# First norm's gain as one row spread by TensorE, a TensorE start at the first microseconds, S5 table loads issued one by one, rotary angles in two steps

## The chip, the cores and the metric

The kernel runs on one core of one Trainium2 chip. The metric is the device time of one execution in microseconds, the median of the runs shown.

## The reference

Two layers of a hybrid decoder trunk on 256 tokens of width 1024, all in float32. What matters here, cut short:

```python
for l in range(2):
    h = _rmsnorm(x, ffn1_norm[l])
    x = x + 0.5 * _swiglu(h, ffn1_w_gate[l], ffn1_w_up[l], ffn1_w_down[l])   # 1024 -> 2816 -> 1024
    h = _rmsnorm(x, mix_norm[l])
    ... = jnp.split(h @ w_in[l], IN_SPLIT_POINTS, axis=-1)                   # 1024 -> 12288
    y_a = _hgrn2(...); y_b = _s5(...); y_c = _conformer_conv(...); y_d = _dilated_attention(...)
    merged = sum over k of gates[:, :, k] * (y_k @ w_branch[l, k])
    x = x + merged @ w_out[l]
    h = _rmsnorm(x, ffn2_norm[l])
    x = x + 0.5 * _swiglu(h, ffn2_w_gate[l], ffn2_w_up[l], ffn2_w_down[l])
return _rmsnorm(x, final_norm)

def _rmsnorm(x, gain):
    return x * lax.rsqrt(jnp.mean(x * x, axis=-1, keepdims=True) + 1e-6) * gain
```

The S5 mixer needs, per layer, tables made from its parameters alone (powers of the diagonal state matrix, `b` and `c` folded into them); the attention's partial rotary embedding needs cosines and sines of position times 16 frequencies.

## The kernel before

**Work and stages.** The 256 tokens are two row tiles of 128. TensorE multiplies activations by 270 MB of weights, streamed once. A float32 weight slot of 128x1024 elements arrives in a buffer `raw`; ScalarE rounds it to a high part `whi`, VectorE forms the rest `wlo`; each activation is split the same way (`hTh`, `hTl`), and each product is the sum of three matmuls, `hi*hi`, `hi*lo` and `lo*hi` (`mm3`). One slot is used by 12 matmuls of 512 columns or 24 of 256. `Stream` keeps up to 4 loads (`NRAW`) and 5 slots (`NW`) split ahead of TensorE. Weight loads are issued on SyncE's queue (SP, L139).

**What sets the order.** All is written into the engines' streams by one Python program, in order. `Paced` adds up estimated times for each engine as instructions are written; side jobs (generators: `prepare`, the S5 tables, the mixers) are advanced by `tick` between matmuls where those estimates leave room. A side job's bare `yield` lets it go on once TensorE's estimated time has caught up with what the job wrote; `yield n` waits at least 2.6 us times n of that time; `yield GO` lets it go on at once if there is room. So a change of a yield or of an instruction moves side jobs among the matmuls of one feed-forward stage.

**The start.** SP loads `x[0]` in two halves (L391), then `gain0`, the first norm's gain repeated over 128 partitions by a zero-stride read (`load_gain`, L403), then two loads of the gate weights, `x[1]` (L408) and two more. `norm.square` squares and sums on ScalarE, `norm.rows` makes the scale `var` (GpSimd's power) and on VectorE `xn = x * var * gain`, in two halves of 512 columns; `norm.turn` transposes `xn` on TensorE into `xT`, which ScalarE and VectorE split into `hTh` and `hTl`; then the gate product (`gate_t`) of the first row tile goes over the four slots of the first 512 columns. The second row tile is normed between them, on the same engines.

**Side jobs in the first feed-forward.** `prepare` turns parameter columns, makes masks, the rotary angles `ang` (32 VectorE instructions of one column each) and the S5 constants. Then `s5_turns` (`ctab`, `stab`) and `s5_tables(l)`: seven loads issued by ScalarE without a yield between them (`braw` L632, `craw` L634, `draw` L635), then on VectorE `pows`, `bb`, `b` and `C4`, on TensorE transposes and small products `s5k`, and at last `K4` (named `K`, 20 instructions from `s5k`, then two additions). The second layer does its tables in its own first feed-forward. `K4` is first used by `s5()` in the mixers, whose products are `yk`.

PSUM's mixed banks (`mx_bank`, `tr_bank`: four buffers under one tag) hold transposes and side jobs' products; four others (`acc_bank`) the main products.

Of the kernel before, what the change touches and what calls it, by code (L numbers as in the profile page):

```python
# [16 lines left out]
ALU = mybir.AluOpType  # L17
AX = mybir.AxisListType

P = 128  # L20
DM = 1024
# [11 lines left out]
GO = -1  # L33
# [155 lines left out]
def trunk(ctx, tc, x_in, positions, ffn1_norm, ffn1_w_gate, ffn1_w_up, ffn1_w_down, mix_norm, w_in,  # L189
# [3 lines left out]
    nc = tc.nc  # L193
    V, S, T, G = (Paced(nc.vector, dve_cost), Paced(nc.scalar, ActCost()), Paced(nc.tensor, pe_cost),
                  Paced(nc.gpsimd, pool_cost))
# [5 lines left out]
    def const(shape, name, dtype=F32):  # L201
        return sb.tile(shape, dtype, tag=name, name=name, bufs=1)

    def H(shape, name, dtype=F32):
        return sb.tile(shape, dtype, tag="heap", name=name, bufs=NHEAP)

    def H2(shape, name, dtype=F32):
        return sb.tile(shape, dtype, tag="half", name=name, bufs=NHALF)
# [9 lines left out]
    def mx_bank(name):  # L218
        return ps.tile([P, 512], F32, tag="mx", name=name, bufs=4)

    def tiny(shape, name, bufs=4):
        return sb.tile(shape, F32, tag=name, name=name, bufs=bufs)
# [163 lines left out]
    ident = const([P, P], "ident")  # L386
    make_identity(nc, ident)

    x = [const([P, DM], f"x{t}") for t in range(2)]
# [3 lines left out]
    gain_src = []  # L393
# [3 lines left out]
    gains = {}  # L397

    def load_gain(n):
        if n < len(gain_src) and n not in gains:  # L400
            g = H([P, DM], f"gain{n}")
            src = gain_src[n]
            (nc.scalar if n else nc.sync).dma_start(g, bass.AP(tensor=src.tensor, offset=src.offset, ap=[[0, P], [1, DM]]))  # L403
            gains[n] = g

    load_gain(0)
    ws.load(2)
    nc.sync.dma_start(x[1], x_in[0, P:2 * P, :])  # L408
    ws.load()
# [69 lines left out]
    def prepare():  # L479
# [40 lines left out]
        pcol = tiny([P, 2], "pcol", 1)  # L520
        V.tensor_copy(pcol, b[:, :2])

        inv = np.float32(500000.0) ** (-np.arange(16, dtype=np.float32) / np.float32(16))
        ang = H2([P, 2, 2, 16], "ang")
        for i in range(16):
            for t in range(2):
                V.tensor_scalar(ang[:, t, 0, i:i + 1], pcol[:, t:t + 1], float(inv[i]), None, op0=ALU.mult)
            if i % 4 == 3:
                yield GO
        V.tensor_scalar(ang[:, :, 1, :], ang[:, :, 0, :], math.pi / 2, None, op0=ALU.add)  # L530

        red = H2([P, 2, 16], "red")
        src = H2([P, 2, 16], "angc")
# [27 lines left out]
        def t5(name):  # L561
            if name in ("mag", "cth", "sth", "zr", "zi"):
                return const([P, 32], "s5" + name)
            return t5t[:, t5n.setdefault(name, len(t5n)), :]
# [8 lines left out]
        hs, hc, ab = t5("hs"), t5("hc"), t5("ab")  # L573
# [47 lines left out]
    def s5_tables(l):  # L621
# [8 lines left out]
        draw = tiny([16, 2, 16], "draw", 1)  # L630
        for k, (bs, cs) in enumerate(((s5_b_re, s5_c_re), (s5_b_im, s5_c_im))):
            nc.scalar.dma_start(braw[:, k], bs[l].rearrange("(j g) p c -> (g p) j c", g=2))  # L632
            for g in range(2):
                nc.scalar.dma_start(craw[k][:, :, g, :], cs[l].rearrange("(a g) c p -> (g c) a p", a=4))  # L634
        nc.scalar.dma_start(draw, s5_d[l].rearrange("(a h c) -> h a c", a=2, c=16))  # L635
        yield

# [33 lines left out]
        for half in range(2):  # L671
            hs = slice(4 * half, 4 * half + 4)
# [34 lines left out]
        for half in range(2):  # L707
            hs = slice(8 * half, 8 * half + 8)
# [47 lines left out]
        for g in range(2):  # L756
            bv = kb[g].rearrange("p (h s c) -> p s h c", h=8, s=4)
            for i in range(4):
                for i0 in range(i + 1):
                    if i0 == 0:  # L760
                        V.tensor_scalar(K4v[:, g, i], bv[:, i], mi[:, 0:1], None, op0=ALU.mult)
                    else:
                        V.scalar_tensor_tensor(K4v[:, g, i], bv[:, i - i0], mi[:, i0:i0 + 1], K4v[:, g, i],
                                               op0=ALU.mult, op1=ALU.add)
            yield GO
        for half in range(2):
            hs = slice(8 * half, 8 * half + 8)
# [6 lines left out]
    def s5_turns(l):  # L774
# [11 lines left out]
        def square(i):  # L786
# [4 lines left out]
            V.scalar_tensor_tensor(d[:, 1], c_, 2.0, s_, op0=ALU.mult, op1=ALU.mult)  # L791
            return 1 - i
        i = square(square(i))
        G.memset(ctab[:, :, 0:1], 1.0)
        G.memset(stab[:, :, 0:1], 0.0)
        yield
        n = 1
        while n < 64:
            cb, sb_ = (e[i][:, k, :, None].to_broadcast([P, 16, n]) for k in range(2))
            for k, op in ((0, ALU.subtract), (1, ALU.add)):  # L800
                u1, u2 = H2([P, 16, 32], "u1"), H2([P, 16, 32], "u2")
                V.tensor_tensor(u1[:, :, :n], ctab[:, :, :n], (cb, sb_)[k], op=ALU.mult)
                V.tensor_tensor(u2[:, :, :n], stab[:, :, :n], (sb_, cb)[k], op=ALU.mult)
                V.tensor_tensor((ctab, stab)[k][:, :, n:2 * n], u1[:, :, :n], u2[:, :, :n], op=op)
                if n > 4:
                    yield GO
            n *= 2
            if n < 64:
                i = square(i)
            yield GO  # L810
# [98 lines left out]
    class Norm:  # L909
# [10 lines left out]
        def square(self, t, h):  # L920

            hs = slice(512 * h, 512 * h + 512)
            if h == 0:
                self.ss[t] = tiny([P, 2], "ss")
                self.xn[t] = H([P, DM], f"xn{self.n}_{t}")
            S.activation(H2([P, 512], "junk"), x[t][:, hs], AF.Square, scale=1.0 / 32.0, accum_out=self.ss[t][:, h:h + 1])
            if self.final:
                V.tensor_tensor(self.xn[t][:, hs], x[t][:, hs], gains[self.n][:, hs], op=ALU.mult)

        def rows(self, t):  # L930
            ss, xn = self.ss.pop(t), self.xn[t]
            var = tiny([P, 2], "var")
            V.scalar_tensor_tensor(var[:, 0:1], ss[:, 0:1], EPS, ss[:, 1:2], op0=ALU.add, op1=ALU.add)
            G.tensor_tensor(var[:, 1:2], var[:, 0:1], neghalf, op=ALU.pow)
            for h in range(2):
                hs = slice(512 * h, 512 * h + 512)
                if not self.final:
                    V.scalar_tensor_tensor(xn[:, hs], x[t][:, hs], var[:, 1:2], gains[self.n][:, hs],
                                           op0=ALU.mult, op1=ALU.mult)
                elif h == 0:  # L940
                    V.tensor_scalar(xn[:, hs], xn[:, hs], var[:, 1:2], None, op0=ALU.mult)
                else:
                    S.activation(xn[:, hs], xn[:, hs], AF.Copy, scale=var[:, 1:2])
                if self.final:
                    (nc.sync, nc.scalar)[h].dma_start(out[0, t * P:(t + 1) * P, hs], xn[:, hs])
            if t == 1:
                del gains[self.n]
# [85 lines left out]
    class Tail:  # L1033
# [5 lines left out]
        def half(self, t, h, acc, scale):  # L1039
            if t == 0 and h == 0:  # L1040
                self.norm = Norm(self.final)
                load_gain(self.norm.n)
            hs = slice(512 * h, 512 * h + 512)
            V.scalar_tensor_tensor(x[t][:, hs], acc, scale, x[t][:, hs], op0=ALU.mult, op1=ALU.add)
            self.norm.square(t, h)
            if h == 1:
                self.norm.rows(t)
# [565 lines left out]
    ws.high()  # L1613
    load_rows()
    g_prep = start(prepare(), -2)
    for l in range(DEPTH):
        def tables(l=l):
            while g_prep in side:
                yield
            turns = start(s5_turns(l), -1)  # L1620
            step(turns)
            yield from s5_tables(l)
            while turns in side:
                yield
        g_tab = start(tables(), -2)
        for i, phase in enumerate((ffn, mixers, ffn)):
            tail = Tail(final=(l == DEPTH - 1 and i == 2))
            if phase is mixers:
                finish(g_prep)
                mixers(l, norm, tail, g_tab)  # L1630
            else:
                ffn(norm, tail)
            norm = tail.norm
# [31 lines left out]
```

## Time and profile before

| | |
|---|---|
| median of 3 runs | 1583.33 us (1577.35, 1583.33, 1583.43) |
| profiled execution, its own time | 1577.96 us |
| its span | 1576.3 us |
| TensorE busy (matmul) | 1550.6 us, 98% of the span |
| VectorE, ScalarE, GpSimd busy | 1106.4, 839.6, 28.1 us |
| granted TensorE clock, mean | 0.998 |
| HBM read | 277.53 MB, 178 GB/s over the span |

A timeline row gives start, duration (both us), engine, source line, operation, output<-inputs, shapes and count; in brackets the engine's idle time before it and what ended that. Nearly every instruction passes through one helper, so its line is L72 and the tile names tell what it is. PE is TensorE, DVE VectorE, ACT ScalarE, POOL GpSimd; "ACTq" and "SPq" are DMA issues in those engines' streams.

### The profile page before, as it was taken

The numbers are of one execution on the slowest core, as the hardware profiler recorded it, in microseconds if no ns is written. First come the engines' busy times: TensorE is split into PE (matmuls) and PEld (weight loads), VectorE is DVE, ScalarE is ACT, GpSimd is POOL, SyncE is SP. The second block draws the span as 40 slices with busy tenths as digits, with TensorE's granted clock in tenths as the row PEclk, the third lists the DMA queues.
The fourth block names the chain that finished last, engine by engine and source line by source line (L and its number), as shares of the span: only waits on it lengthen the run. The fifth ranks groups of instructions, "written<-read, shape, count | busy, mean of one in ns | idle before, by whom it ended". The sixth has DMA issues, their size and how long they took to land.

```text
span 1576.3 us, 27619 instructions
## 1 busy us (share of the span) xinstructions
PE 1550.6 (98%) x11407; PEld 1417.4 (90%) x11407; DVE 1106.4 (70%) x1797; ACT 839.6 (53%) x1209; POOL 28.1 (2%) x58
## 2 busy tenths in 40 slices
PE   7999999999999999999999999999999999999998
PEld 5999789889899998999889988987899999989986
DVE  6778865976878866555478874568768897765553
ACT  5545555567565465444445543656665555554442
POOL 2000000000000000000000000000000000000000
PEclk9999999999999999999999999999999999999999
DMA  7565556553544556555565555665345445655551
GB/s 275 198 173 200 194 179 204 161 173 122 161 161 161 170 184 222 188 189 212 174 180 188 188 187 191 206 193 172 116 150 171 160 161 178 211 183 181 188 207 56
DMA packets 179518, 282.46 MB, mean 179 GB/s; under 512 B 26718, under 2 KB 82080, under 8 KB 179392
## 3 DMA queue, kind: packets, MB, share of 16 engines
q1 hardware_dynamic: 154240, 270.55, 51.4%
q10 hardware_dynamic: 24832, 9.97, 2.6%
q8 instruction: 89, 1.46, 0.4%
q14 instruction: 37, 0.30, 0.1%
q0 software_dynamic: 320, 0.18, 0.0%
HBM read 277.53 MB, written 3.15 MB: 178 GB/s over the span
## 4 chain that ended last, share of the span: by engine, by line
PE 91%; DVE 3%; ACT 2%; ACTq 1%; DMA 1%; issue 1%; POOL 0%; SPq 0%; POOLq 0%; DVEq 0%
PE down L72 15%; PE up_h L72 12%; PE gate_h L72 12%; PE att_t L72 11%; PE pgt_h L72 11%; PE br L72 6%; PE po_t L72 3%; PE gate_t L72 3%; PE up_t L72 2%; PE pi_t L72 1%; PE pb_h L72 1%; PE pu_h L72 1%; PE pf_h L72 1%; PE pa_h L72 1%; PE glu L72 1%; PE hl L72 1%
## 5 line engine op out<-in xcount | busy, mean ns | idle before, releaser
L72 DVE TENSOR_TENSOR wlo<-raw,whi 128x1024 fp32r<-128x1024 f32 x512 | 614.8, 1220 | 194.0 <-ACT whi L72 98.8
L72 ACT ACTIVATE whi<-raw 128x1024 fp32r<-128x1024 f32 x512 | 526.2, 1055 | 180.5 <-PE down L72 97.5
L72 PE MATMUL gate_h<-hTh,wlo 128*128 128x256 f32 x576 | 160.2, 278 | 2.8 <-DVE wlo L72 2.8
L72 PE MATMUL gate_h<-hTh,whi 128*128 128x256 f32 x576 | 161.1, 280 | 0.0
L72 PE MATMUL up_h<-hTh,whi 128*128 128x256 f32 x576 | 160.8, 279 | 0.2 <-ACT whi L72 0.2
L72 PE MATMUL up_h<-hTh,wlo 128*128 128x256 f32 x576 | 160.0, 278 | 0.8 <-DVE wlo L72 0.8
L72 PE MATMUL up_h<-hTl,whi 128*128 128x256 f32 x576 | 160.0, 278 | 0.0
L72 PE MATMUL gate_h<-hTl,whi 128*128 128x256 f32 x576 | 159.9, 278 | 0.0
L72 PE MATMUL pgt_h<-hTh,whi 128*128 128x256 f32 x512 | 145.6, 284 | 0.0
L72 PE MATMUL pgt_h<-hTl,whi 128*128 128x256 f32 x512 | 142.6, 279 | 0.0
L72 PE MATMUL pgt_h<-hTh,wlo 128*128 128x256 f32 x512 | 142.6, 279 | 0.0
L72 PE MATMUL down<-whi,gh 128*128 128x512 f32 x352 | 138.8, 394 | 0.0
L72 PE MATMUL down<-whi,gl 128*128 128x512 f32 x352 | 138.6, 394 | 0.0
L72 PE MATMUL down<-wlo,gh 128*128 128x512 f32 x352 | 138.2, 393 | 0.0
L72 PE MATMUL att_t<-whi,hTh 128*128 128x512 f32 x288 | 117.7, 409 | 0.0
L72 PE MATMUL att_t<-whi,hTl 128*128 128x512 f32 x288 | 113.5, 394 | 0.0
L72 PE MATMUL att_t<-wlo,hTh 128*128 128x512 f32 x288 | 113.0, 392 | 0.0
L72 PEld LDWEIGHTS gate_h<-hTh,wlo 128*128 128x128 f32 x576 | 108.2, 188 | 3.4 <-DVE wlo L72 3.4
L72 PEld LDWEIGHTS up_h<-hTh,whi 128*128 128x128 f32 x576 | 108.9, 189 | 0.6 <-ACT whi L72 0.4
L72 PEld LDWEIGHTS up_h<-hTh,wlo 128*128 128x128 f32 x576 | 108.1, 188 | 1.0 <-DVE wlo L72 1.0
L72 PEld LDWEIGHTS gate_h<-hTh,whi 128*128 128x128 f32 x576 | 108.8, 189 | 0.1
L72 PEld LDWEIGHTS gate_h<-hTl,whi 128*128 128x128 f32 x576 | 108.2, 188 | 0.0
(385 smaller groups left out, 3333.1 us busy)
## 6 DMA issues: line engine op xcount, KB each, us to landing
raw<-in_w_in_dram SPq DMA_DIRECT2D x60, 1024.0 KB, 5.1
raw<-in_ffn_w_up_dram SPq DMA_DIRECT2D x44, 1024.0 KB, 5.3
raw<-in_ffn_w_down_dram SPq DMA_DIRECT2D x44, 1024.0 KB, 4.9
raw<-in_ffn_w_gate_dram SPq DMA_DIRECT2D x42, 1024.0 KB, 5.1
raw<-in_w_in_dram SPq DMA_DIRECT2D x72, 512.0 KB, 4.7
raw<-in_w_branch_dram SPq DMA_DIRECT2D x16, 1024.0 KB, 5.1
raw<-in_w_out_dram SPq DMA_DIRECT2D x8, 1024.0 KB, 5.2
raw<-in_s_w_glu_dram SPq DMA_DIRECT2D x16, 256.0 KB, 3.8
```

Source lines behind the costliest of these rows:

```text
L72: return f(*args, **kw)
```

## The change

The first norm's gain is loaded as one row of 1x1024 (`grow`), issued by ScalarE as its first instruction; a row of ones times it, on TensorE, writes the gain of all 128 partitions to two PSUM banks, from which VectorE reads it in `norm.rows`. Ahead of that TensorE multiplies the identity by itself four times (`wake`, its result is not used). The 16 frequencies are set by GpSimd, and the angles are two VectorE instructions instead of 32. Between the S5 tables' loads stands a `yield 2`.

```diff
-            (nc.scalar if n else nc.sync).dma_start(g, bass.AP(tensor=src.tensor, offset=src.offset, ap=[[0, P], [1, DM]]))
-            gains[n] = g
-
-    load_gain(0)
+            nc.scalar.dma_start(g, bass.AP(tensor=src.tensor, offset=src.offset, ap=[[0, P], [1, DM]]))
+            gains[n] = [g[:, 512 * h:512 * h + 512] for h in range(2)]
+
+    grow = H([1, DM], "grow")
+    nc.scalar.dma_start(grow, bass.AP(tensor=gain_src[0].tensor, offset=gain_src[0].offset, ap=[[0, 1], [1, DM]]))
+    ones = H2([1, P], "ones")
+    G.memset(ones, 1.0)
+    wake = mx_bank("wake")
+    for i in range(4):
+        T.matmul(wake[:, P * i:P * i + P], ident, ident, start=True, stop=True)
+    gains[0] = [mx_bank(f"gain0_{h}") for h in range(2)]
+    for h in range(2):
+        T.matmul(gains[0][h], ones, grow[:, 512 * h:512 * h + 512], start=True, stop=True)
     ws.load(2)
...
         ang = H2([P, 2, 2, 16], "ang")
+        freq = H2([P, 16], "freq")
         for i in range(16):
-            for t in range(2):
-                V.tensor_scalar(ang[:, t, 0, i:i + 1], pcol[:, t:t + 1], float(inv[i]), None, op0=ALU.mult)
-            if i % 4 == 3:
-                yield GO
+            G.memset(freq[:, i:i + 1], float(inv[i]))
+        for t in range(2):
+            V.tensor_scalar(ang[:, t, 0, :], freq, pcol[:, t:t + 1], None, op0=ALU.mult)
+        yield GO
...
             nc.scalar.dma_start(braw[:, k], bs[l].rearrange("(j g) p c -> (g p) j c", g=2))
+            yield 2
             for g in range(2):
                 nc.scalar.dma_start(craw[k][:, :, g, :], cs[l].rearrange("(a g) c p -> (g c) a p", a=4))
+                yield 2
...
-                    V.scalar_tensor_tensor(xn[:, hs], x[t][:, hs], var[:, 1:2], gains[self.n][:, hs],
+                    V.scalar_tensor_tensor(xn[:, hs], x[t][:, hs], var[:, 1:2], gains[self.n][h],
```

The order moves at three places. The first is TensorE's stream at the very start; before, it began with the transposes of the normed rows:

```order
L72 MATMUL xT_00_146<-ident,xn_0_130 128x128 x4
L72 MATMUL xT_01_153<-ident,xn_0_130 128x128 x4
L72 MATMUL gate_t_191<-whi_140,hTh_0_112 128x512
L72 MATMUL gate_t_191<-wlo_142,hTh_0_112 128x512
L72 MATMUL gate_t_191<-whi_140,hTl_0_114 128x512
```

With the change:

```order
L72 MATMUL wake<-ident 128x128 x4
L72 MATMUL gain_0_83<-grow,ones 128x512
L72 MATMUL gain_1_84<-grow,ones 128x512
L72 MATMUL xT_00_157<-ident,xn_0_141 128x128 x4
L72 MATMUL xT_01_164<-ident,xn_0_141 128x128 x4
L72 MATMUL gate_t_202<-whi_151,hTh_0_123 128x512
```

Six products stand ahead of the transposes; the rest of the start keeps its order on every engine, and SP's stream has lost the gain's load between `x[0]` and the first weights.

The second is ScalarE's stream in the first layer's first feed-forward, where the tables' loads are issued. Before, all seven stand together between two roundings of weights (`whi`):

```order
L72 ACTIVATE sg_1079<-gate_h_1026 128x512
L72 ACTIVATE whi_1083<-raw_835 128x1024
L632 DMA braw<-in_s_b_re_dram 128x16x16
L634 DMA craw_1121<-in_s_c_re_dram 128x4x64 x2
L632 DMA braw<-in_s_b_im_dram 128x16x16
L634 DMA craw_1122<-in_s_c_im_dram 128x4x64 x2
L635 DMA draw<-in_s_d_dram 16x2x16
L72 ACTIVATE whi_1147<-raw_867 128x1024
L72 ACTIVATE sg_1190<-gate_h_1085 128x512
```

With the change, the first three of them:

```order
L643 DMA braw<-in_s_b_re_dram 128x16x16
L72 ACTIVATE gh_737<-sg_871 128x512
L72 ACTIVATE whi_1047<-raw_833 128x1024
L72 ACTIVATE whi_1078<-raw_875 128x1024
L72 ACTIVATE sg_1118<-gate_h_1051 128x512
L72 ACTIVATE whi_1122<-raw_833 128x1024
L646 DMA craw_1024<-in_s_c_re_dram 128x4x64
L72 ACTIVATE whi_1168<-raw_875 128x1024
L72 ACTIVATE sg_1208<-gate_h_1124 128x512
L72 ACTIVATE whi_1214<-raw_985 128x1024
L72 ACTIVATE whi_1248<-raw_1045 128x1024
L646 DMA craw_1024<-in_s_c_re_dram 128x4x64
```

Each load now has three or four roundings of weights between it and the next, and the seven stretch over 19 slots of weights; what VectorE makes of them begins 19 slots later than before (`pows` after the 50th `wlo` instead of the 31st), and `s5_turns` moves ahead into the gap.

The third is the end of the tables on VectorE, the making of `K4` (`K`). Before, in the first layer's down projection, its two halves stood a slot of weights apart, and its additions came 9 slots later:

```order
L72 TENSOR_TENSOR wlo_2269<-raw_2005,whi_2239 128x1024
L72 TENSOR_SCALAR K_1115<-s5k_2048,mi 128x8x16 x2
L72 SCALAR_TENSOR_TENSOR K_1115<-s5k_2048,mi,K_1115 128x8x16
L72 TENSOR_SCALAR K_1115<-s5k_2048,mi 128x8x16
L72 SCALAR_TENSOR_TENSOR K_1115<-s5k_2048,mi,K_1115 128x8x16 x2
L72 TENSOR_SCALAR K_1115<-s5k_2048,mi 128x8x16
L72 SCALAR_TENSOR_TENSOR K_1115<-s5k_2048,mi,K_1115 128x8x16 x3
L72 TENSOR_TENSOR wlo_2297<-raw_2044,whi_2273 128x1024
```

With the change, in the mixers' third product (`pf`), the end of the second half and what follows it:

```order
L72 TENSOR_SCALAR K_1018<-s5k_2418,mi 128x8x16
L72 SCALAR_TENSOR_TENSOR K_1018<-s5k_2418,mi,K_1018 128x8x16 x3
L72 TENSOR_TENSOR wlo_2678<-raw_2381,whi_2629 128x1024
L72 TENSOR_TENSOR u_2694<-dcol,diag 128x512
L72 TENSOR_TENSOR K_1018<-K_1018,u_2694 128x512
L72 TENSOR_TENSOR u_2697<-dcol,diag 128x512
L72 TENSOR_TENSOR K_1018<-K_1018,u_2697 128x512
L72 TENSOR_SCALAR kT<-kT 128x512
L72 TENSOR_SCALAR lf<-lf 128x512
L72 TENSOR_TENSOR wlo_2718<-raw_2393,whi_2680 128x1024
```

All 20 pieces of `K` now stand in one run between two `wlo`, 14 slots of weights later than before, and the additions follow after one more. From the mixers' later stages on, VectorE's order is the same as before, until the second layer's first feed-forward, where the tables move alike.

## Rows read from the trace of the kernel before

**Rows 1.** The page's busy times.

```profile
PE 1550.6 (98%) x11407; PEld 1417.4 (90%) x11407; DVE 1106.4 (70%) x1797; ACT 839.6 (53%) x1209; POOL 28.1 (2%) x58
```

**Rows 2.** Waits of PE: total us, times, longest us.

```profile
PE xT L72 <- DVE xn L72: 9.1, 1, 9.1
PE gate_h L72 <- DVE wlo L72: 2.8, 2, 2.1
```

**Rows 3.** Timeline of the start, all engines.

```profile
1.08 0.29 POOL masks.py:199 TENSOR_SCALAR_AFFINE_SELECT ident<-ident 128x128 f32<-128x128 f32 x1
...
5.50 0.55 POOL L72 TENSOR_TENSOR var<-var,neghalf 128x1 f32<-128x1 f32 x1 [3.74 <-DVE var L72]
8.28 1.41 DVE L72 SCALAR_TENSOR_TENSOR xn<-x,var,gain 128x512 f32<-128x512 f32 x2 [2.94 <-DMA gain<-in_ffn_norm_dram]
...
9.09 1.97 PE L72 MATMUL xT<-ident,xn 128*128 128x128 f32 x8 [9.09 <-DVE xn L72]
9.48 1.06 ACT L72 ACTIVATE whi<-raw 128x1024 fp32r<-128x1024 f32 x1 [4.33 <-DMA raw<-in_ffn_w_gate_dram]
...
16.46 0.63 PE L72 MATMUL gate_t<-whi,hTl 128*128 128x512 f32 x1
...
17.47 0.51 PE L72 MATMUL gate_t<-wlo,hTh 128*128 128x512 f32 x1
...
18.05 0.39 PE L72 MATMUL gate_t<-whi,hTh 128*128 128x512 f32 x1
```

**Rows 4.** DMA issues: count, KB each, median us from issue to landing.

```profile
gain<-in_ffn_norm_dram SPq DMA_DIRECT2D x1, 512.0 KB, 6.4
...
draw<-in_s_d_dram ACTq DMA_DIRECT2D x2, 2.0 KB, 2.5
```

**Rows 5.** Timeline of PE, three float32 products of 256 columns.

```profile
359.24 1.46 PE L72 MATMUL as<-ak,aq 128*128 128x256 f32 x6
```

**Rows 6.** Timeline of ACT, first layer, the S5 tables' loads.

```profile
89.11 3.17 ACTq L634 DMA_DIRECT2D craw<-in_s_c_re_dram  x1
...
94.28 5.01 ACTq L634 DMA_DIRECT2D craw<-in_s_c_im_dram  x2
99.33 0.52 ACTq L635 DMA_DIRECT2D draw<-in_s_d_dram  x1
99.89 1.06 ACT L72 ACTIVATE whi<-raw 128x1024 fp32r<-128x1024 f32 x1 [9.72 <-issue]
```

**Rows 7.** Timeline of PE just after those loads.

```profile
101.23 0.28 PE L72 MATMUL up_h<-hTl,whi 128*128 128x256 f32 x1
102.27 0.39 PE L72 MATMUL up_h<-hTh,wlo 128*128 128x256 f32 x1 [0.76 <-DVE wlo L72]
...
107.60 0.28 PE L72 MATMUL gate_h<-hTh,whi 128*128 128x256 f32 x1
107.72 0.28 PE L72 MATMUL gate_h<-hTl,whi 128*128 128x256 f32 x1
110.13 0.38 PE L72 MATMUL gate_h<-hTh,wlo 128*128 128x256 f32 x1 [2.14 <-DVE wlo L72]
```

**Rows 8.** Timelines of ACT and PE, second layer, the same loads and what follows.

```profile
813.00 4.85 ACT L72 ACTIVATE whi<-raw 128x1024 fp32r<-128x1024 f32 x5 [9.15 <-DMA craw<-in_s_c_re_dram]
...
822.42 0.39 PE L72 MATMUL gate_h<-hTh,wlo 128*128 128x256 f32 x1 [0.69 <-DVE wlo L72]
...
825.71 0.63 PE L72 MATMUL b<-ident,b 128*128 128x128 f32 x4 [0.52 <-DVE b L72]
```

**Rows 9.** Groups by line and form: busy us, mean ns, idle before.

```profile
L72 ACT ACT_TABLE_LOAD x51 | 65.4, 1283 | 17.9 <-DMA raw<-in_w_in_dram 16.3 <-PEq L1651 0.8
...
L72 DVE TENSOR_SCALAR ang<-pcol 128x1 f32<-128x1 f32 x32 | 2.1, 144 | 0.0
```

**Rows 10.** The tile K: duration in ns min/median/max.

```profile
L72 DVE SCALAR_TENSOR_TENSOR K<-s5k,mi,K x24: 349/351/355, 190.1 to 935.1; 128x128 f32<-128x128 f32 x24
...
L72 DVE TENSOR_TENSOR K<-K,u x4: 691/692/693, 222.7 to 938.6; 128x512 f32<-128x512 f32 x4
```

More of the change, by code (lines that the diff above doesn't have):

```diff
@@ L927, in square @@
             if self.final:
-                V.tensor_tensor(self.xn[t][:, hs], x[t][:, hs], gains[self.n][:, hs], op=ALU.mult)
+                V.tensor_tensor(self.xn[t][:, hs], x[t][:, hs], gains[self.n][h], op=ALU.mult)
         def rows(self, t):
```

## The prediction

> **What bounds the kernel.** I read the page's busy times first: TensorE computes in 98% of the span [rows 1], so nothing but its idle time, or its slow time, can be won, some 26 us in all. The list of its waits tells where: 9.1 us before its first instruction, and 2.8 us in two waits for `wlo` in the gate products [rows 2]. The timeline of the start then shows what the first wait is made of [rows 3]: the norm's scale `var` is there at 5.50 + 0.55 = 6.05, but `xn` starts at 8.28, since the gain has only just landed; issued at 1.71, it took 6.4 us [rows 4]. The first weights land after it (`whi` at 9.48 waited for `raw` [rows 3]). [...] At 17.47 TensorE waits for the third slot's `wlo`, which VectorE makes after the second row tile's norm. From 17.47 on it runs with hardly a gap until about 100 us, so **17.47 is the moment that the start's saving is measured at**, and what is won before it and not at it is nothing.
>
> The other two waits stand behind the S5 tables' loads. ScalarE's stream is held by their issue: one takes 3.17 us, two 5.01, although a single one can take 0.52, and the next `whi` comes after 9.72 us without work [rows 6]. TensorE lives on its split slots, then waits: 102.27 instead of soon after 101.23, and 110.13 instead of 107.83 [rows 7]. In the second layer the block is 9.15 us, and TensorE waits 0.69 and 0.52 [rows 8].
>
> **The gain's way (start).** Removed: 512 KB from SP's queue ahead of the weights. From the gain's landing (1.71 + 6.4 = 8.1) to the first weights' (9.48) are 1.4 us for the same 512 KB; without the gain the weights come that much after `x[0]` instead, well before 8, and are no longer last. Added: one row of 4 KB. The nearest row is `draw`, 2 KB, 2.5 us to landing [rows 4]; issued as its engine's first instruction, at about 1, it is there by 3.7. Upper bound: the gain's own 6.4 us, so 7.4. ScalarE's issue stands ahead of its table load, and it then waits for `x[0]` in any case.
>
> On TensorE, three float32 products of 256 columns take 1.46 us at full pace [rows 5], 1.9 ns per column. So four `wake` products of 128 cost 1.0 us, at half pace 2.0, from 1.4, when `ident` is made (1.08 + 0.29 [rows 3]): done at 3.4 at the latest, before the row. The two gain products of 512 columns cost 1.0 us each, at half pace 1.95: from 3.7 they end at 5.7 or 7.6. `xn`'s halves are 0.7 us each; the first starts with `var` at 6.1, the second at 6.8 or, at half pace, 7.6. So `xn` ends at 7.5 or 8.3, where it ended at 8.28 + 1.41 = 9.69: **1.4 to 2.2 us earlier**. At full pace the eight transposes would also lose half of their 1.97 us, some 0.4 of it after `xn`'s end, which makes 2.6. From `xn` to the wait at 17.47 the chain is the same work on the same engines (transposes, two splits, a rounding, two squares, the second norm, its `wlo`).
>
> TensorE was at half pace for 7.8 us after its first product (9.09 to past 16.88, of which 16.46 is a row [rows 3]); the same from 1.4 ends at 9.2. That is the nearest row, so I take half pace for the gain products and a little of the transposes for the better: **-1.5**. Bounds: -2.6, and +2.1, if the row is as late as the gain was: products from 7.4 to 11.3 at half pace, `xn` ending at about 11.8 instead of 9.69.
>
> [...] By the rows, half pace ended once and nothing after 18.05 in the start fell back. [...]
>
> VectorE reads the gain from PSUM now; 0.7 us a half is taken for that too. Three of four mixed PSUM banks are held until the second `xn`; the transposes that need the next bank wait for that `xn` anyway.
>
> **The angles.** 32 instructions, 2.1 us of VectorE [rows 9], become 2; 16 memsets go to GpSimd, busy 28 us of the span [rows 1]. TensorE does not wait there: nothing. As a result the scheduler places `prepare` a little earlier and needs three more table loads on ScalarE, 1.28 us each [rows 9], all in its idle time; uncovered they would cost 3.8.
>
> **The loads one by one.** The seven issues stay; each has three or four `whi` between it and the next, so they come some 5 us apart, and I price an issue at the 0.52 of `draw` [rows 6]; upper bound 3.17. Even that is one issue between roundings, covered by up to five split slots. What goes: in the first layer 102.27 - 101.23 and 110.13 - 107.72, less the 0.12 that lies between two products (107.60, 107.72) each: 0.92 + 2.29 = **-3.2**. The second layer's two, 0.69 + 0.52 = 1.2 [rows 8]; but `s5_turns` now crowds into those first slots of VectorE, so **-1.0**, bounds 0 and -1.4. What is late next: the tables themselves, by up to 19 slots; their last additions were in the mixers even before, so only the last rival hangs on that.
>
> **Sum.** -1.5 - 3.2 - 1.0 = -5.7. The profiled execution has 1577.96, so **1572.3 us**. The median of the runs shown is 1583.33, 5.4 above it: two of three lie at 1583.4 and one at 1577.35, a step of 0.35% that the one trace cannot explain. If the median after lies on the upper level, it is 1577.8.
>
> **Rivals.** [...]
>
> *The S5 wait comes back elsewhere.* VectorE's table work crowds into other slots; TensorE waits there as long as before. For it: the work is the same and merely moved. Against it: what blocked was ScalarE's stream, not VectorE. Start alone: 1576.5.
>
> *It doesn't do what it says.* An issue takes as long alone as in a row, and the row lands no earlier than the weights did: 1578.
>
> *The run of `K`* (the other side). Twenty pieces at 0.35 and four instructions at 0.69 [rows 10] are 9.8 us of VectorE with one `wlo` among them. TensorE uses up a slot in 24 products 0.12 apart [rows 7], 2.8 us. With s slots ahead at the first piece it waits 9.8 - 2.8 s, once in each layer: nothing with four, 1.4 with three, 4.2 with two. The sum turns where twice that wait is 5.7, at two and a half slots; with two it is 8.4 - 5.7, so 1580.7 against 1577.96. Against it: before, ten pieces in a row cost nothing, and the job starts only where VectorE is little behind.
>
> *The row is late*: +2.1 - 4.2: 1575.9.
>
> **How the numbers follow.** Forecast 0.57, wake in vain 0.13, S5 wait elsewhere 0.13, nothing 0.07, late row 0.06, `K` 0.04. A measurement of this kernel can tell about 0.5%, 7.9 us. The likeliest is 1572.3. Range 1568 to 1579: below, all lower bounds together (-2.6 - 3.5 - 1.4, so 1570.5) and some scatter; above, the upper level of the runs with the forecast (1577.8) or the weak cases on the lower. Against the median of 1583.33, faster by over 0.5% is below 1575.4: the lower level (about half) in the forecast or with `wake` in vain, some 0.38, and 0.07 for a gain of over 7.9 on the upper: 0.45. Slower by over 0.5% needs the run of `K` with a slot less on the upper level, 0.04 at most. Within 0.5%: 0.51.
>
> **What would show it.** TensorE's first product at about 1.4; `xn` at 6.1, released by GpSimd or TensorE and not by a DMA; the `wlo` that was waited for at 17.47 at about 16. Seven issues of half a us in ScalarE's stream with roundings between, and no wait for `wlo` near 100 or 820. The forecast is wrong if `xn` waits for the gain's products past 8, if TensorE's products after 16 still last 0.63, or if a new wait for `wlo` of over 2 us stands anywhere, above all behind `K`.

## The result and the profile after

In the first comparison the kernel before took 1583.38 us (median of four, 1577.35 to 1583.66) and the change 1565.95 (1563.96 to 1568.48): a ratio of 0.990, interval 0.987 to 0.993, faster by 16 us where 5.7 were forecast and outside the range given. Repeated on two other chips the change was at 0.992 (0.989 to 0.995) and 0.992 (0.990 to 0.994) of before, 9 to 17 us. The profiled executions, 1577.96 and 1563.96 us, have spans of 1576.3 and 1562.3, 14.0 apart.

The page's busy times, with TensorE a little less busy than in [rows 1]:

```profile
PE 1548.3 (99%) x11419; PEld 1413.7 (90%) x11419; DVE 1104.7 (71%) x1767; ACT 843.4 (54%) x1212; POOL 28.0 (2%) x75
```

The timeline of the start, all engines (columns as in [rows 3]):

```profile
1.43 2.08 PE L72 MATMUL wake<-ident 128*128 128x128 f32 x8 [1.43 <-POOL ident masks.py:199]
...
3.44 3.78 PE L72 MATMUL gain<-grow,ones 1*128 1x512 f32 x4
...
5.87 0.55 POOL L72 TENSOR_TENSOR var<-var,neghalf 128x1 f32<-128x1 f32 x1 [3.99 <-DVE var L72]
6.46 1.54 DVE L72 SCALAR_TENSOR_TENSOR xn<-x,var,gain 128x512 f32<-128x512 f32 x2 [0.74 <-POOL var L72]
...
7.26 1.97 PE L72 MATMUL xT<-ident,xn 128*128 128x128 f32 x8
7.88 1.06 ACT L72 ACTIVATE whi<-raw 128x1024 fp32r<-128x1024 f32 x1 [2.35 <-DMA raw<-in_ffn_w_gate_dram]
...
9.47 0.80 PE L72 MATMUL gate_t<-whi,hTh 128*128 128x512 f32 x1 [0.24 <-ACT hTh L72]
...
15.28 0.63 PE L72 MATMUL gate_t<-whi,hTh 128*128 128x512 f32 x1
15.86 0.64 PE L72 MATMUL gate_t<-wlo,hTh 128*128 128x512 f32 x1
16.34 0.40 PE L72 MATMUL gate_t<-whi,hTl 128*128 128x512 f32 x1
```

`xn` starts at 6.46 behind GpSimd's `var` instead of at 8.28 behind the gain, the weights land 1.6 us earlier, and the `wlo` that TensorE waited for is used at 15.86 instead of 17.47 [rows 3]: 1.61 us won, 1.5 forecast. The half pace (products of 512 columns 0.43 us from start to start, 0.23 from 16.34 on; eight transposes 1.97 us at 7.26, 1.03 at 17.27), which the prediction let end at 9.2, lasted until 16.34, although TensorE was at work from 1.43 on: up to 15.86 its timeline has one wait, of 0.24 us, and from start to start three pauses of 0.2 to 0.35 us between 9.4 and 11.5.

ScalarE's timeline at the S5 loads, two of the seven, which answer to [rows 6]:

```profile
92.80 0.37 ACTq L646 DMA_DIRECT2D craw<-in_s_c_re_dram  x1
93.12 1.06 ACT L72 ACTIVATE whi<-raw 128x1024 fp32r<-128x1024 f32 x1
...
130.79 0.39 ACTq L648 DMA_DIRECT2D draw<-in_s_d_dram  x1
131.20 1.05 ACT L72 ACTIVATE whi<-raw 128x1024 fp32r<-128x1024 f32 x1
```

And the list of TensorE's waits (total us, times, longest), where the waits for `xn` and `wlo` of [rows 2] no longer stand:

```profile
PE hl L72 <- DVE KL L72: 3.2, 2, 1.6
PE wake L72 <- POOL ident masks.py:199: 1.4, 1, 1.4
PE rt L72 <- ACT ak L72: 0.9, 2, 0.4
PE gate_t L72 <- ACT hTh L72: 0.8, 3, 0.3
```

Taken from start to start of TensorE's products, the waits near 101 and 108 us [rows 7] were 3.6 us, those near 822 and 825 [rows 8] 1.5; all are gone. With the start that makes 6.7 us, one more than forecast. It is half of the 14.0.

**The other half** is in products that wait for nothing. They are float32r products (those of `whi`, `wlo`, `hTh`, `hTl`; `fp32r` in the rows), and they run at one of two paces. In the last feed-forward, whose order is the same, 24 products of before (first row to last) take 2.83 us, 117.8 ns each:

```profile
1450.04 0.28 PE L72 MATMUL up_h<-hTh,whi 128*128 128x256 f32 x1
...
1452.87 0.28 PE L72 MATMUL gate_h<-hTh,whi 128*128 128x256 f32 x1
```

and with the change 2.72, 113.3 each:

```profile
1450.03 0.28 PE L72 MATMUL gate_h<-hTh,whi 128*128 128x256 f32 x1
...
1452.75 0.28 PE L72 MATMUL up_h<-hTh,whi 128*128 128x256 f32 x1
```

Both run at the full granted clock (1.00 from 1450 to 1453 us in both profiles). Products of 512 columns differ by as much, 229 or 233 ns. Summed over all pairs of neighbours in the trace, the time above 113.3 and 229 ns, called the excess from here on, is 11.7 us before and 3.2 after. Against that 8.5, the granted clock fell to half once more after than before (3.4 us at half, 1.7 lost). 6.7 + 8.5 - 1.7 is 13.5 of the 14.0. The lower pace begins and ends mostly at handovers, where a float32 product (a transpose, an S5 or attention product) is followed by float32r products, and mostly holds until the next one: of the stretches between two float32 products with at least eight distances of 256 columns within 2 ns of either pace, over nine tenths of these distances are at one pace in 65 of 86 before and in 73 of 84 after.

The sum closes in the other executions traced of the two kernels too. Span, less excess, less what the falls of the clock cost ahead of the end, is 1576.3 - 11.7 - 1.7 = 1562.9 and, in a second trace, 1570.1 - 8.1 - 0 = 1562.0 for before; for the change it is 1555.7, 1555.4 and 1555.9. These are 6.8 apart in the mean, the size of the waits. So of all that differs between the traces only the waits are the same each time; excess and clock vary from execution to execution.

### The profile page after: what moved, and what is told of

The parts are those of the page before. It is cut to its first block, busy times and chain, and to the rows that moved or that the text cites. A ratio compares the mean times of both kernels' runs of the same rounds, so it can differ in the third digit from the quotient of the medians.

```text
span 1562.3 us, 27640 instructions
## 1 busy us (share of the span) xinstructions
PE 1548.3 (99%) x11419; PEld 1413.7 (90%) x11419; DVE 1104.7 (71%) x1767; ACT 843.4 (54%) x1212; POOL 28.0 (2%) x75
## 4 chain that ended last, share of the span: by engine, by line
PE 96%; ACT 1%; DVE 1%; issue 1%; DMA 1%; POOL 0%; ACTq 0%; SPq 0%; POOLq 0%; DVEq 0%
PE down L72 15%; PE gate_h L72 13%; PE up_h L72 13%; PE att_t L72 12%; PE pgt_h L72 11%; PE br L72 6%; PE gate_t L72 3%; PE up_t L72 3%; PE po_t L72 3%; PE pi_t L72 1%; PE pu_h L72 1%; PE pb_h L72 1%; PE pg_t L72 1%; PE pa_h L72 1%; PE glu L72 1%; PE pq_h L72 1%
## 5 line engine op out<-in xcount | busy, mean ns | idle before, releaser
L72 PEld LDWEIGHTS up_h<-hTl,whi 128*128 128x128 f32 x576 | 108.1, 188 | 0.0
```

What stands on the lines that cost most here:

```text
L72: return f(*args, **kw)
```

## Experiments

All ratios are to the kernel before on the same chip, whose medians were 1573.9 to 1580.1 on five chips (17 to 29 executions each). A ratio is estimated from all executions; it is not the quotient of the two medians beside it.

| kernel | median us | before there | ratio, 95% interval |
|---|---|---|---|
| before again | 1576.5 | 1576.2 | 1.001 (0.999, 1.003) |
| before + three banks | 1572.2 | 1576.2 | 0.999 (0.997, 1.000) |
| change + one bank | 1568.7 | 1576.2 | 0.995 (0.993, 0.997) |
| before + yields | 1578.1 | 1576.2 | 1.001 (0.999, 1.003) |
| change again | 1568.1 | 1580.1 | 0.992 (0.989, 0.995) |
| change, loads in a row | 1570.1 | 1580.1 | 0.994 (0.992, 0.997) |
| change, old angles | 1577.2 | 1580.1 | 0.998 (0.996, 1.000) |
| change, no wake | 1565.8 | 1580.1 | 0.991 (0.988, 0.993) |
| before + small buffer | 1575.7 | 1573.9 | 1.000 (0.999, 1.002) |
| change, ones of its own | 1569.1 | 1573.9 | 0.997 (0.994, 0.999) |
| before + angles | 1569.1 | 1573.9 | 0.998 (0.996, 0.999) |
| before + start | 1570.1 | 1578.0 | 0.996 (0.994, 0.997) |
| change, third time | 1564.9 | 1578.0 | 0.992 (0.990, 0.994) |
| before + calm | 1574.8 | 1578.0 | 0.998 (0.997, 1.000) |
| before + calm, again | 1577.4 | 1576.0 | 1.000 (0.998, 1.002) |
| change + calm | 1563.4 | 1576.0 | 0.991 (0.989, 0.994) |
| no wake, `hl` later | 1557.0 | 1573.9 | 0.989 (0.987, 0.991) |
| the same, again | 1561.8 | 1578.0 | 0.991 (0.989, 0.993) |

**Does the pace repeat?** The kernel before and the change once more, unchanged.

> The kernel before, unchanged. In the trace of before, TensorE's float32r products of 256 columns start 113.3 ns apart in most stretches, but 117.8 ns apart in some, among them the whole last feed-forward from 1405 to 1559 us; over all products the excess above the quicker pace is 11.7 us, against 3.2 in the trace of the change. Theory A (the pace is fixed by the program): the same stretches are slow again, the last feed-forward too, and the excess is 10 to 14 us. Theory B (it is drawn anew in each execution): other stretches are slow, and the excess differs by several us from 11.7.

> The change, unchanged. The runs so far put before at a median of 1576.2 us over 26 executions (1570.8 to 1580.6), not 1583.4, and in two profiled executions of one and the same kernel the long feed-forward stretches were once at 117.8 ns a product and once at 113.3. Theory B (the pace of a long stretch is drawn in each execution, alike for both kernels): only the waits count, so 1576.2 - 6.7 = 1569.5 us median, with a spread of some 8 us like before's. Theory C (something in the change makes the quick pace the rule): 1565 to 1567, spread under 5 us, and an excess over 113.3 ns of 3 to 5 us in the trace where before has 8 to 12.

Theory A fell for the two long stretches, the second feed-forward of each layer. From the last transposes `gT` to the last product, before needed

```profile
1406.85 0.60 PE L72 MATMUL gT<-ident,sg 128*128 128x128 f32 x4
...
1568.80 0.39 PE L72 MATMUL down<-whi,gl 128*128 128x512 f32 x1
```

and before again

```profile
1405.43 0.60 PE L72 MATMUL gT<-ident,sg 128*128 128x128 f32 x4
...
1562.61 0.39 PE L72 MATMUL down<-whi,gl 128*128 128x512 f32 x1
```

161.95 and 157.18 us, the same instructions. The change again had the slow one, 4.95 more than the first time. The other long stretch (second feed-forward of the first layer) has the same two lengths, 4.8 to 4.9 us apart. Over the twenty traces of this section and the comparison one of the two was slow in eight, never both: some five us of an execution's time are drawn, that is, differ between executions of one program. The median of the change again came where theory B had it apart from its chip (1568.1, spread 6.4); the ratio did not.

The falls of the clock are not what sets before and the change apart. Every execution has its mean granted clock on record (to three digits, so only means are of use). Span times what the clock lacks of 1 is 4.2 and 5.1 us in the mean for before, on the chips of the change again and of its third run, and 3.7 and 4.4 us for the change there: 0.5 and 0.6 of the 13.0 us between the mean spans. Less the waits' 6.7, some 5.7 us are left, which by the sums above can only be excess; for executions without a trace that is argued.

The shorter stretches do repeat. In the mixers' gate stage (`pgt`, 134 us) most handovers came out alike in every execution and both layers, and differently in before and in the change. What sets them was the next question.

**PSUM banks?** Idle products at the start turn the four mixed banks by three (before) and by one (change):

```diff
     load_gain(0)
+    for k in range(3):
+        T.engine.matmul(mx_bank(f"turn{k}")[:, :P], ident, ident, start=True, stop=True)
```

> Before, with three idle products of the identity at the start, each into a mixed PSUM bank of its own, so that all later transposes and side products stand three banks (of four) further, as in the change; order and SBUF as in before. TensorE waits there anyway, so they cost nothing. Theory A1 (the pace after a run of float32 products hangs on the bank they wrote): the slow stretches become those of the change, the last feed-forward is at 113.3 ns, and the time falls by 4 to 9 us from before's 1583.4. Theory A2 (it hangs on SBUF addresses): nothing moves there, so the time stays within 1.5 us of before. Theory B (drawn in each execution): no steady difference.

> The change, with one more idle product into a mixed bank at the start, so that its later transposes stand on the same banks as in before. Theory A1: the slow stretches of before come back in the later stages where the order is the same (the last feed-forward at 117.8 ns), and the time rises from the change's 1566 by 4 to 9 us. A2 and B: within 1.5 us of 1566.

Neither pattern moved, but for single handovers: A1 fell. The last feed-forward of before with three banks was quick, the other long stretch slow. The change with one bank lay 5 to 12 us under before on its chip, beside the change's 9 to 17 on others, with the change's pattern and an excess of 4.3 us in its trace; why it is less is not shown.

**Places in SBUF?** The change takes `ones` from the half-size pool before the first weights are loaded; thereby the pool lies at 119 KB and `raw` behind it, in before the other way round.

```diff
     load_gain(0)
+    ones = H2([1, P], "ones")
+    G.memset(ones, 1.0)
```

> Before with one small buffer of ones from the half-size pool, allocated and set by GpSimd at the start and never used. The order on every other engine is unchanged; but the pool now lies at 119 KB of SBUF and the weights' raw buffers behind it at 140 KB, as in the change, instead of the other way round. In the ten traces so far the pace after most handovers from float32 to float32r products is one of two patterns: one in all kernels with before's place of these buffers, another in all with the change's. Theory L (this place sets the pattern): the pattern becomes the change's (the product after ydT starts 207 ns behind and goes on at 113.3 ns, where before 201 and 117.8), and the time falls by 2 to 5 us against before. Theory G (the gain's own way does it, or the queues): the pattern stays before's and the time is that of before within 1 us.

```diff
-    ones = H2([1, P], "ones")
+    ones = const([1, P], "ones")
```

> The change with the row of ones in a buffer of its own instead of one of the half-size pool; order unchanged, and raw buffers and half-size pool lie as in before (512 bytes further). Theory L: before's pattern comes back, and the time rises by 2 to 5 us above the change (1568.1 on the chip of its repeat, 1566 in its first runs). Theory G: the change's pattern and time stay, within 1 us.

The patterns followed the places both ways. 24 products behind `ydT` in the first layer: before,

```profile
522.40 0.28 PE L72 MATMUL pgt_h<-hTh,wlo 128*128 128x256 f32 x1
...
525.23 0.28 PE L72 MATMUL pgt_h<-hTh,wlo 128*128 128x256 f32 x1
```

before with the small buffer,

```profile
521.81 0.28 PE L72 MATMUL pgt_h<-hTh,wlo 128*128 128x256 f32 x1
...
524.52 0.28 PE L72 MATMUL pgt_h<-hTh,wlo 128*128 128x256 f32 x1
```

the change with `ones` of its own,

```profile
518.72 0.28 PE L72 MATMUL pgt_h<-hTh,wlo 128*128 128x256 f32 x1
...
521.54 0.28 PE L72 MATMUL pgt_h<-hTh,wlo 128*128 128x256 f32 x1
```

and the change itself,

```profile
517.55 0.28 PE L72 MATMUL pgt_h<-hTh,wlo 128*128 128x256 f32 x1
...
520.27 0.28 PE L72 MATMUL pgt_h<-hTh,wlo 128*128 128x256 f32 x1
```

2.83, 2.71, 2.82 and 2.72 us. Over the whole gate stage of a layer the excess is 1.6 to 2.0 us in the eight traces with before's places and 0.8 in the twelve with the change's, without an exception. Outside the two long stretches it is 6.0 to 8.3 us in the eight and 3.2 to 5.3 in the twelve: some 3 us. So that the places set the pattern is shown; which buffer's place does it, the pool's or `raw`'s, was not tried. That they make the time is not: the small buffer left before's time within -2.4 and +2.8 us, not the 2 to 5 less that were expected (its profiled execution had a slow long stretch), while `ones` of its own left the change at -5.2 (-8.8 to -1.7) against before, the size of the removed waits alone, but on another chip than the change's own runs.

**The parts by themselves.** Yields alone, angles alone, start alone, and the change without each:

> Before with the yields between the S5 tables' loads alone. By the prediction's sum: -4.2 us (3.2 in the first layer, 1.0 in the second), about 1579 against 1583.4. A rival: the changed order also moves TensorE's pace, by as much as some 8 us either way; then the difference is off by what the excess over 113.3 ns says in its trace.

> Before with the angles in two VectorE instructions alone. The prediction gave this part 0. The change without the yields between the loads still lost the two waits near 101 and 108 us, and the change with the old angles gained new ones at 242 and 325. Theory: the angles' shorter job alone takes the first layer's two waits away, -2 to -3.6 us, and leaves the second layer's at 821 and 825. Rival: it needs the start too; then the waits near 101 and 108 stay, and 0.

> Before with the change's start alone (the gain as one row, its products, wake), without the yields and with the old angles. By the prediction -1.5 us: the third slot's wlo at about 16 instead of 17.5, the waits near 101, 108, 821 and 825 us as before. Rival: the change of place of the half-size pool, which comes with it, moves the pace too, by up to 3 us either way.

> The change without the yields between the S5 tables' loads. By the prediction's step the waits near 100, 108 and 820 us come back: +4.2 to +5.1 us against the change. Rival (with the angles in two steps the tables start elsewhere anyway): less than 2 us. The pace may add up to 5 us either way; the trace says how much.

> The change with the angles in 32 VectorE instructions as before. The prediction's step gave the angles nothing: 0 us. Rival, from the run of before with the yields alone, where the late tables made TensorE wait 2.8 us ahead of s5k at 243 us and 1.3 us more at 325: the angles' shorter job is what gives the tables their place in the order, so without it these waits come back, +3 to +5 us.

The yields alone won nothing in time. The first layer's waits near 101 and 108 went, and the list of waits shows what came:

```profile
PE hl L72 <- DVE KL L72: 4.4, 2, 2.9
PE s5k L72 <- ACT BA L72: 3.0, 2, 2.8
```

Their loads last until 149 us, the change's until 131, and the tables are then late for `s5k` and `hl`. The change with the old angles has the same two waits:

```profile
PE hl L72 <- DVE KL L72: 4.5, 2, 2.8
PE s5k L72 <- ACT BA L72: 2.9, 1, 2.9
```

and behind the wait for `s5k` the clock falls, by the stretches of its profile (us; busy us and count per engine; PEclk is the granted clock, DMA share and GB/s):

```profile
244.60:251.40 6.80, 6.46 (x54) 6.16 (x55) 5.81 (x14) 5.18 (x11) 0.00 (x0) 0.50 0.79 264
252.00:262.00 10.00, 10.00 (x120) 8.78 (x120) 9.62 (x16) 3.17 (x5) 0.00 (x0) 1.00 0.15 44
```

6.8 us at half clock cost 3.4. Its three falls together cost 8.5, and a long stretch was slow: its span is 1576.5. Its median is 9.1 us above the change's on the same chip, where the prediction's step had 0 and the rival 3 to 5. The angles alone took both waits near 101 and 108 away (its list has `xn` 9.4, `hl` 3.2 and one `wlo` of 0.7, in the second layer), and its time fell by 1 to 6 us. Their job ends sooner, so that the seven loads stand nine us earlier, and even in a row they hold ScalarE only from 79.33 to 84.76:

```profile
79.33 0.44 ACTq L633 DMA_DIRECT2D braw<-in_s_b_re_dram  x1
79.81 1.15 ACTq L635 DMA_DIRECT2D craw<-in_s_c_re_dram  x1
...
84.10 0.66 ACTq L636 DMA_DIRECT2D draw<-in_s_d_dram  x1
```

Accordingly the change with its loads in a row has no wait behind them in the first layer, and the second layer's two (0.68 and 0.52) come back; its median is 2.0 us above the change's, not the 4.2 to 5.1 of the prediction's step. The start alone had its wait for `wlo` end at 15.43, one of the first layer's waits (2.1) and both of the second's; its time, 4 to 10 us under before, is more than its 2 to 3 us of waits, as the new places of the buffers would have it.

**Wake.**

```diff
-    wake = mx_bank("wake")
-    for i in range(4):
-        T.matmul(wake[:, P * i:P * i + P], ident, ident, start=True, stop=True)
```

> The change without the four products of wake; the rest of the order is the same. Theory 'in vain': TensorE's products at the start are at half pace until 16 to 17 us with and without them, so 0 us, within 0.5. Theory 'it wakes': the gain products and transposes lose up to 0.7 us. Its banks stand one further back; by the run with one bank more this moves the pace by less than 3 us.

Without it the row has landed by 2.39, the gain's products start a microsecond earlier, and full pace comes at 12.12, not later. TensorE's timeline:

```profile
2.39 3.75 PE L72 MATMUL gain<-grow,ones 1*128 1x512 f32 x4 [2.39 <-DMA grow<-in_ffn_norm_dram]
...
11.80 0.48 PE L72 MATMUL gate_t<-wlo,hTh 128*128 128x512 f32 x1
12.12 0.39 PE L72 MATMUL gate_t<-whi,hTl 128*128 128x512 f32 x1
...
15.07 0.50 PE L72 MATMUL gate_t<-wlo,hTh 128*128 128x512 f32 x1 [1.65 <-DVE wlo L72]
```

What the start is measured at, the third slot's `wlo`, comes at 15.07 here, and at 15.7 and 16.0 in two traces of a later kernel without `wake`; in nine traces with `wake` at 15.4 to 16.3. The time, 1565.8 beside the change's 1568.1, is inside the spread of both. So `wake` was in vain as far as these runs tell. In the change's first trace TensorE was at half pace without a gap from 1.43 through the transposes at 7.26, and had not been at full pace before. The first product at full pace came at 11.2 to 16.3 us in the nine traces with `wake`, at 12.1 to 15.0 in the three without. In the four of these twelve in which TensorE paused once ahead of it between its first gate products it came by 12.1, in the eight with three pauses at 12.5 or later; that the pauses do it is not shown.

**Can the pace be forced?** An unused float32 product of 256 columns behind the last `gT`:

```diff
                             T.transpose(b[:, i * P:(i + 1) * P], g[:, i * P:(i + 1) * P], ident)
+                        if t == 1 and norm.n in (2, 5):
+                            T.engine.matmul(mx_bank("calm")[:, :2 * P], ident, x[0][:, :2 * P], start=True, stop=True)
```

> Before with one unused float32 product of 256 columns behind the transposes gT of the second row tile in each layer's second feed-forward, the last float32 product for some 155 us; nothing else moves. In all fourteen traces the handover behind such a product (as2, 305 ns to the next but one) went on at 113.3 ns a product, while behind gT the long stretches (632 to 788 and 1407 to 1559 us) were at 117.8 in 6 of 28. Theory B2 (the long stretches' pace is drawn at that one handover and makes much of the runs' spread): both stretches are at 113.3, the runs that lie 5 to 10 us above the fastest go, and the median falls by 0.5 to 4 us although the two products cost 0.5 us each. Rival: the spread comes from falls of the clock behind hl or from elsewhere; spread and median stay, the latter within 1 us.

> Before with the two unused products behind gT, again, now as the ground for the next kernel: median 3 to 4 us below before's on the same chip where before's runs spread over 10 us or more, and a spread of its own under 6 us.

> The change with the same two products, beside before with them on one chip, so that the two long stretches are at 113.3 ns in both. If the waits and the short stretches are all that the change won, the medians lie 6.7 + 1.5 to 2 = 8 to 9 us apart (7 to 10 with the clock's falls). If something else in the change is worth more, 11 us or more; if the rest was the long stretches' luck alone, 6 to 7.

The first run looked like a success: 1571.6 to 1576.0 beside 1571.0 to 1584.5. The repeat refuted it: 1572.6 to 1584.6, and in its trace the last feed-forward is slow behind the new product. Since the pace was not forced, the 14 us between it and the change with the same products (1562.5 to 1565.1) don't separate the draw from the rest. On the same chip the change with them lay 12.6 us under before's median; 11 or more was to mean that something beyond the waits and the short stretches is won, and no run tells what.

**A version that beats both.** Two waits stood in every trace, `hl` for `KL`, and behind them the granted clock mostly fell to half (25 of 36 times in eighteen traces). Without `wake`, and with a yield ahead of `hl`:

```diff
                                   b.rearrange("p (a t) -> p a t", a=4))
                 drop()
+            yield 1
```

> The change without wake, and with a yield of one before the products hl, which in every trace wait 1.5 to 1.7 us for KL (323 and 1094 us) and behind which the granted clock falls to half for 3.4 or 6.8 us in most traces. Expected: both waits and those falls of the clock go: 3.2 us and 1.7 to 6.8 us, so 1558 to 1563 against the change's 1566 to 1568. Rival: the later products push the mixers' next steps into a new wait, and nothing is won.

> The change without wake and with the yield before hl, again, beside the change on one chip: 6 to 10 us under the change, with a spread of under 4 us, since its granted clock does not fall behind hl.

> The change, unchanged, beside the next kernel on one chip. By the waits that its traces lack, 6.7 us less than before; by the two comparisons so far, 12 to 17 us. If the rest is drawn, it lands between: 7 to 12 us under the median of before.

The change a third time lay 13.1 us under before's median, a little more than the 7 to 12 expected. In the new version the waits for `KL` are gone, and the clock stays whole. Stretches of the change around the two waits:

```profile
325.50:331.50 6.00, 6.00 (x28) 5.09 (x28) 6.00 (x9) 1.58 (x2) 0.00 (x0) 0.72 0.52 175
...
1098.00:1102.00 4.00, 4.00 (x13) 3.13 (x13) 4.00 (x7) 1.58 (x2) 0.00 (x0) 0.57 0.80 262
```

and of this version:

```profile
325.00:332.00 7.00, 7.00 (x42) 6.08 (x41) 6.97 (x12) 4.31 (x14) 0.00 (x0) 1.00 0.64 224
1090.00:1102.00 12.00, 12.00 (x68) 10.27 (x67) 11.71 (x18) 9.14 (x20) 0.00 (x0) 1.00 0.79 276
```

It took 1556.0 to 1558.2 on one chip and 1556.9 to 1563.3 on another, where the change took 1561.6 to 1567.1: 3.1 us between the medians, not the 6 to 10 expected, and a spread of 6.5, not under 4. Its profiled execution there had the first long stretch slow (4.9 us), which its first profile had not.

## Why the prediction was wrong

- **"Nothing but its idle time, or its slow time, can be won, some 26 us in all."** This is the step that failed. The slow time was looked for in the granted clock alone, and a product's duration was taken as given wherever that clock was whole. Two paces, 4.4 ns apart on some 9250 pairs of products, held 11.7 us of the profiled time of before and 3.2 of the change's, all of it inside "busy". The views read for idle time can't show this; the mean durations by tile do, faintly (`gate_h` with `wlo` 278 ns before, 276 after).
- **The size.** -5.7 was forecast; the waits alone gave -6.7 (1.6, 3.6 and 1.5), which on their own would still have been near the forecast. By the traces some 3 us of excess go with the new places of the buffers. What is left of the 9 to 17 us measured, 2 to 3 us of the 13.0 on two chips, lies hardly in the falls of the clock (0.5 and 0.6 us). It could be the draw of the long stretches, but the traces don't show that the change shifts it: 3 of 16 were slow with before's places, 5 of 24 with the change's. That part of the cause stays open.
- **The median's upper level**, which the text could not explain, is of the size of a long stretch drawn slow: 4.7 us in the trace of before alone, which is on the lower level. No trace of an execution on the upper level was compared, so this is argued.
- **The start**: right, 1.6 for 1.5, at the place named and for the reason given: `xn` no longer waits for the gain, and the weights land earlier. Over the traces the third slot's `wlo` comes at 15.4 to 16.3 us with the new start, at 17.1 to 18.1 in the seven with the old one. One term of it failed without harm: half pace was to last 7.8 us from the first product, so to 9.2, and lasted until 16.34. For `wake` in vain, 0.13 of the chances, no run shows that half pace takes from the saving: it lasted past the moment measured, and the start still won its 1.6 us; without `wake` the median was 1565.8 beside 1568.1, inside the spread of both.
- **The loads**: right in sum (3.6 for 3.2, 1.5 for 1.0), wrong in cause. The rival that the wait comes back elsewhere is what the yields alone do in the first layer. A second step, "TensorE does not wait there: nothing" for the angles, failed here: 2 us of VectorE's time were rightly free, but the shorter job moves the loads and the tables in the order. That the first layer's share came out is luck: the yields alone gave new waits, 2.8 us for `s5k` and 1.3 us more for `hl`. With the old angles the change keeps only 0 to 7 us of its gain.
- **The run of `K`** cost nothing: no wait for `wlo` stands behind it.

## What to carry to other kernels

Count a busy engine's time per product, not only its gaps: group start-to-start distances of equal products, and compare the same instructions in two executions of one kernel before giving a difference to a change. A change that allocates a buffer or shortens a side job also moves later addresses and places in the order (here the half-size pool and `raw`, with some 3 us of excess, and the S5 loads, by nine us); run its parts alone, and the kernel with only the allocation. A short wait of a nearly full TensorE cost more than itself here: behind 25 of the 36 waits of `hl`, 1.5 to 2.9 us long, the granted clock fell to half for 3.4 or 6.8 us, 1.7 or 3.4 us lost.

## What was not expected of the hardware

- Equal float32r products with no wait between them ran 113.3 or 117.8 ns apart at 256 columns, 229 or 233.4 at 512, at the full granted clock (1.00 from 1410 to 1558 us, at the slower level in before, at the quicker in the change). The level was mostly taken at a handover from float32 products and kept (65 of 86 stretches before, 73 of 84 after), in the long stretches for some 160 us (157.2 or 162.0).
- At many handovers the level followed where buffers lie in SBUF (excess of a gate stage 1.6 to 2.0 us in the eight traces with before's places, 0.8 in the twelve with the change's); turning the PSUM banks of the float32 results, by three in before and by one in the change, did not move it but for single handovers. At the long stretches it differed between executions of one kernel (161.95 and 157.18 us for before). The mechanism stays open.
- Behind waits of 1.5 to 2.9 us the granted clock fell to half for 3.4 or 6.8 us, but not each time: behind 25 of the 36 waits of `hl` for `KL` in eighteen traces. Before again kept it whole through both of its.
- One DMA issue of the tables in ScalarE's stream took 0.37 to 0.43 us with roundings between; seven in a row took 11.2 us in before (88.64 to 99.85), 5.4 us where the angles' part moved them nine us earlier. Why is not shown.
